# Griffin and dilated-attention encoder in one kernel: gate weights on GpSimd's queue and loaded earlier, side transfers at estimated ends, a table load counted

## The chip, the cores and the metric

The kernel runs as one launch on one core of a Trainium2 chip. The metric is the device time of the launch in microseconds, the median of several runs. The core has five queues that take instructions in order: PE (TensorE, the matrix unit), ACT (ScalarE), DVE (VectorE), POOL (GpSimd) and SP, which only issues transfers here. POOL issues transfers too. SBUF is the on-chip memory of 128 partitions, PSUM the eight banks that PE writes.

## The reference

An encoder trunk of two layers on x of 512 tokens by 1024 channels, in float32. Layer 0 mixes tokens with a recurrent block, layer 1 with dilated window attention; a gated feed-forward block with a 3-tap convolution follows each. The change touches layer 0's mixer alone:

```python
def rglru_mixer(x, w_in, conv_w, conv_b, w_a, b_a, w_x, b_x, lam, w_out):
    gate, u = jnp.split(x @ w_in, 2, axis=-1)               # 1280 channels each
    u = depthwise_conv(u, conv_w, conv_b, LRU_CONV_W // 2)  # 4 taps over tokens
    ub = u.reshape(B, S, LRU_BLOCKS, LRU_BLOCK_W)           # 16 blocks of 80 channels
    h_fwd = rglru_scan(u, ub, w_a[0], b_a[0], w_x[0], b_x[0], lam[0], False)
    h_bwd = rglru_scan(u, ub, w_a[1], b_a[1], w_x[1], b_x[1], lam[1], True)
    y = jax.nn.gelu(gate) * (h_fwd + h_bwd).astype(x.dtype)
    return y @ w_out
def rglru_scan(u, ub, w_a, b_a, w_x, b_x, lam, reverse):
    r = jax.nn.sigmoid(jnp.einsum('bsnc,ncd->bsnd', ub, w_a).reshape(B, S, D_RNN) + b_a)
    i = jax.nn.sigmoid(jnp.einsum('bsnc,ncd->bsnd', ub, w_x).reshape(B, S, D_RNN) + b_x)
    log_a = -LRU_C * jax.nn.softplus(-lam.astype(jnp.float32)) * r
    a = jnp.exp(log_a)
    inp = jnp.sqrt(-jnp.expm1(2.0 * log_a)) * (i * u.astype(jnp.float32))
    _, h = lax.associative_scan(lru_combine, (a, inp), axis=1, reverse=reverse)
    return h
```

## The kernel before, in words

**Precision.** Each operand of a matmul is split into a high part (`whi`, `xhi`, rounded) and a low part (`wlo`, `xlo`, the rest), and a product is three passes (`passes`, L270 to L273): high by high, high by low, low by high. A weight tile of 128 by 1024 is loaded raw by SP (`wraw`, L214 or L220); the high part is made by ACT (L184), or, for some tiles, loaded a second time by POOL's queue, which rounds on the way (`rounded`, L212 and L219); the low part is a subtraction on DVE (L189 to L192).

**Units.** The stage works on 1280 channels as ten tiles t of 128. For each there is a unit u (its columns of x @ w_in; 24 matmuls), a unit g (the four gates, forward and backward; one PSUM bank each) and a unit y (the gelu branch, 24 matmuls). `SEQ` (L515) is their order, and with index from 0 it is also the order of their weight tiles:

```python
SEQ = "u0 u1 u2 u3 g0 u4 g1 y0 y1 u5 g2 u6 g3 y2 y3 u7 g4 u8 g5 y4 y5 u9 g6 g7 y6 y7 g8 g9 y8 y9"
```

Then comes the output product with w_out (`token_phase`, L408): ten steps k over y's tiles, each for eight PSUM banks. The first five k run one after the other over all banks (24 matmuls each); the last five are run bank by bank. It needs y's high and low part of tile k (`turned`, L753). After it the feed-forward block starts.

**Gates.** A block of 80 channels doesn't fit a tile of 128, so a gate unit reads its own tile of u and, for the channels that a block shares with the tile before or after, a side operand (`make_side`, L601): some rows of the neighbours' u, copied by SP from SBUF to SBUF, in four or eight small pieces (L608; t mod 5 is 0, 2 or 4, "stacked") or two of 256 KB (L612, L613). It is issued by the low part of the neighbour (`low`, L589), and waits on SP for its source. The gate's weights are a tile of zeros (`zero`, L157, a memset on POOL, for the first three on DVE) into which `add_gates` (L231) copies blocks of w_a and w_x. These pieces wait in `moves`, one deque for each gate; each tick sends one on SP's queue, lowest gate first (`next_move`, L151), and what is left goes at the gate's split (`split_to`, L174).

**How far ahead.** Unit n calls `weights(n)`: tiles up to n + 3 are split, those up to n + 6 are loaded (`RGA = [6, 3]`, L518).

**The planner.** The program is one list for each queue, written by a planner that counts ticks (`tick`, L320) of `TICK` = 0.69 us. A u or y unit has 8 ticks; a gate has 4 if stacked, otherwise 8. Elementwise work is put in as pieces with an engine, a rank, a cost and what they need (`piece`, L287). At each tick `pump` (L300) emits pieces in order of rank, as long as the engine's booked time is at most 1.4 us (`SLK`) ahead of the clock and what they need is due by then. Work outside the pieces is booked where it is emitted: 1.05 for a conversion on ACT, 0.68 for a sigmoid, 0.72 for a tanh, so 4 x 0.68 + 2 x 0.72 = 4.16 us for a gate unit. `need` (L306) emits whatever is left, by rank, until a wanted key is there.

For a tile t the pieces are: rank 0, the convolution (first step on ACT L576, three taps on DVE L581), u's high part on ACT (L587) and low part on DVE (L590), and the gelu of a pair of y units (L727); rank 1, i = i x u on DVE (L658), the exponentials of a pair (L674), squares (L678) and w on DVE (L681), the roots of a pair (L686); rank 2, m, f, b and h on DVE (the input product L689, two scans L694 and L698, their sum L702); rank 3, y's product on DVE (L736), its high part on ACT (L741) and its low part on DVE (L744).

**Tiles.** SBUF work tiles come from an arena of 40 (L36), handed out first in, first out: a new tile waits for the last use of the one that had its place.

At the start of the stage POOL computes the decay rates, a series of some twenty small operations (`decay_rates`, L531).

Of the kernel before, what the change touches and what calls it, by code (L numbers as in the profile page):

```python
# [10 lines left out]
F32 = mybir.dt.float32  # L11
F32R = mybir.dt.float32r
# [10 lines left out]
FIRST = 2  # L23
TURN_AT, TURN_RG = (2, 2), (0, 1)
ZEROED = 3
POOL_LO = True


# [7 lines left out]
class Arena:  # L36
# [16 lines left out]
    def put(self, t):  # L53
        self.free.append(self.of.pop(id(t))[0])
# [3 lines left out]
def encoder(ctx: ExitStack, tc: tile.TileContext, x, ln_g, ln_b, rg_w_in, rg_conv_w, rg_conv_b,  # L58
            rg_w_a, rg_b_a, rg_w_x, rg_b_x, rg_lam, rg_w_out, at_w_qkv, at_w_o, ff_w_up,
            ff_conv_w, ff_conv_b, ff_w_down, out):  # L60
    nc = tc.nc
# [81 lines left out]
    loaders = []  # L143
    raws, his, parts = {}, {}, {}
    rounded = {}
    side_low = set()
    at = {"load": 0, "split": 0}
    gates = []
    moves = {}

# [6 lines left out]
    def zero(j, eng):  # L157
        raws[j] = sb.get([128, 1024], F32, "wraw")
        eng.memset(raws[j], 0.0)

    def load_to(i):
        while at["load"] <= min(i, len(loaders) - 1):
            j = at["load"]
            if j in gates and j not in raws:
                zero(j, nc.gpsimd)
            if j not in raws:
                raws[j] = sb.get([128, 1024], F32, "wraw")
            loaders[j](raws[j])
            if j in rounded:
                his[j] = sb.get([128, 1024], F32R, "whi")  # L170
                rounded[j](his[j])
            at["load"] += 1

    def split_to(i, pool=False):  # L174
        while at["split"] <= min(i, len(loaders) - 1):
# [55 lines left out]
    def add_gates(t):  # L231
        f0 = 128 * t
        blocks = []
        at_row = {tin: (n, row) for n, (tin, row, _) in enumerate(stacked(t) or [])}
        if at_row:
            side_low.add(len(loaders))
        for blk in range(f0 // BW, (f0 + 127) // BW + 1):
            c0, c1 = max(BW * blk, f0), min(BW * blk + BW, f0 + 128)
            for q, tin in ((0, t), (1, t + 1), (1, t - 1)):
                r0, r1 = max(BW * blk, 128 * tin), min(BW * blk + BW, 128 * tin + 128)  # L240
                if r0 < r1:
                    blocks.append((blk, q, r0, r1, tin, c0, c1))

        def go(raw):
            v = raw.rearrange("p (d a q c) -> p d a q c", d=2, a=2, q=2)
            moves[j] = todo = deque()
            for blk, q, r0, r1, tin, c0, c1 in blocks:
                n = r1 - r0
                for a, w in ((0, rg_w_a), (1, rg_w_x)):
                    src = (w[0, :, blk, r0 - BW * blk:r1 - BW * blk, c0 - BW * blk:c1 - BW * blk]  # L250
                           .rearrange("d r c -> r d c"))
                    dst = lambda p, n: v[p:p + n, :, a, q, c0 - f0:c1 - f0]
                    if not (q and at_row):
                        todo.append((dst(r0 - 128 * tin, n), src))
                    elif n == 32:

                        for d in range(2):
                            sd = src[:, d]
                            todo.append((dst(0, 96)[:, d],
                                         bass.AP(tensor=sd.tensor, offset=sd.offset, ap=[[0, 3]] + [list(x) for x in sd.ap])))  # L260
                    else:
                        m, row = at_row[tin]
                        for z in range(3):
                            todo.append((dst(r0 - 128 * tin - row + 16 * m + 32 * z, n), src))

        j = len(loaders)
        gates.append(j)
        loaders.append(go)
# [31 lines left out]
    def pump():  # L300
        now = clock[0] * TICK
        for eng in ("s", "v"):
            while side_work[eng] and booked[eng] <= now + SLK and take(eng, now + SLK):
                pass

    def need(*keys):  # L306
        for key in keys:
            while key not in due:
                assert take("s", 1e9) | take("v", 1e9), key


    queues = []
    later = []
    clock, free_at, gap = [0], [0], [GAP]
    order = itertools.count()
# [4 lines left out]
    def tick():  # L320
        clock[0] += 1
        if moves:
            next_move()
        pump()
        while later and later[0][0] <= clock[0]:
            heapq.heappop(later)[2]()
        if clock[0] >= free_at[0]:
            for q in queues:
                if q and q[0][0](clock[0]):
                    q.popleft()[1]()  # L330
                    free_at[0] = clock[0] + gap[0]
                    return
# [182 lines left out]
    SEQ = "u0 u1 u2 u3 g0 u4 g1 y0 y1 u5 g2 u6 g3 y2 y3 u7 g4 u8 g5 y4 y5 u9 g6 g7 y6 y7 g8 g9 y8 y9"  # L515
    SEQ = [(u[0], int(u[1])) for u in SEQ.split()]
    RTAIL = 5
    RGA = [6, 3]  # L518

    def add_rglru():  # L520
        for kind, t in SEQ:
# [37 lines left out]
    def rglru(i0, turn_params, load_next):  # L559
# [8 lines left out]
        def conv(t, b):  # L568
            if t % 2 == 0:
                u32[t] = u32[t + 1] = sb.get([128, 2, 512], F32, "u32")  # L570
                left[t] = 2
            u = u32[t][:, t % 2]
            c = lambda k: tab[:, k * NR + t:k * NR + t + 1]

            def first():
                nc.scalar.activation(u, b, AF.Identity, bias=tab[:, CB + t:CB + t + 1], scale=c(2))  # L576

            def taps():
                for k, sh in ((0, -2), (1, -1), (3, 1)):
                    d0, d1 = max(0, -sh), 512 - max(0, sh)  # L580
                    nc.vector.scalar_tensor_tensor(u[:, d0:d1], b[:, d0 + sh:d1 + sh], c(k), u[:, d0:d1],  # L581
                                                   op0=OP.mult, op1=OP.add)
                ps.put(b)

            def high():
                uhl[t] = pair("u")
                nc.scalar.activation(uhl[t][:, 0], u, AF.Copy)  # L587

            def low():  # L589
                nc.vector.tensor_tensor(uhl[t][:, 1], u, f(uhl[t][:, 0]), OP.subtract)  # L590
                if t % 5:
                    make_side(t - 1)
                if t % 5 == 4:
                    make_side(t)

            piece("s", 0, 0.76, ("c", t), (), first)
            piece("v", 0, 2.25, ("u", t), (("c", t),), taps)
            piece("s", 0, 0.63, ("uh", t), (("u", t),), high)
            piece("v", 0, 0.69, ("ul", t), (("uh", t),), low)

        def make_side(t):  # L601
# [8 lines left out]
            else:  # L610
                sides[t] = v = pair("side")
                nc.sync.dma_start(f(v[0:64]), f(uhl[t + 1][0:64]))  # L612
                nc.sync.dma_start(f(v[64:128]), f(uhl[t - 1][64:128]))  # L613

        r, ii, th, y = {}, {}, {}, {}
        it = iter(range(i0, i0 + 3 * NR))
        ahead[:] = RGA
# [5 lines left out]

        def g_unit(t):
            need(("ul", max(t - 1, 0)), ("ul", t), ("ul", min(t + 1, NR - 1)))
            sd = sides.pop(t)
            i = next(it)
            v = [w.rearrange("p (m q c) -> p m q c", m=4, q=2) for w in weights(i)]
            r[t] = sb.get([128, 2, 512], F32, "r")
            ii[t] = sb.get([128, 2, 512], F32, "i")  # L630
            th[t] = sb.get([128, 2, 512], F32, "th")
            for m in range(4):
                b = bank("gate")
                passes(b, [w[:, m, 0, :] for w in v], [uhl[t][:, 0], uhl[t][:, 1]], True, False)
                if stacked(t):
                    nc.tensor.matmul(b, v[0][:, m, 1, :], sd, start=False, stop=True)
                else:
                    tick()
                    passes(b, [w[:, m, 1, :] for w in v], [sd[:, 0], sd[:, 1]], False, True)
                tick()  # L640
                d = m // 2
                dst, bias = ((r[t], BA), (ii[t], BX))[m % 2]
                nc.scalar.activation(dst[:, d], b, AF.Sigmoid, bias=tab[:, bias + d * NR + t:bias + d * NR + t + 1])
                book("s", 0.68)
                ps.put(b)
                if m % 2 == 0:
                    nc.scalar.activation(th[t][:, d], r[t][:, d], AF.Tanh, scale=p8[:, d * NR + t:d * NR + t + 1])
                    book("s", 0.72)
            due["g", t] = booked["s"]
            done(i)  # L650
            sb.put(sd)
            if t:
                sb.put(uhl[t - 1])
            if t == NR - 1:
                sb.put(uhl[t])

            def gated():
                nc.vector.tensor_tensor(ii[t], ii[t], u32[t][:, t % 2][:, None, :].to_broadcast([128, 2, 512]), OP.mult)  # L658
                left[t - t % 2] -= 1
                if not left[t - t % 2]:  # L660
                    sb.put(u32[t])

            piece("v", 1, 1.22, ("i", t), (("g", t),), gated)
            if t % 2:
                decay(t - 1, t)
# [97 lines left out]
        load_next()  # L763
        for kind, t in SEQ[FIRST:]:
            {"u": u_unit, "g": g_unit, "y": y_unit}[kind](t)
        i = next(it, i0 + 3 * NR)
        xt.clear()
        load_x()
# [510 lines left out]
```

## Time and profile before

| | |
|---|---|
| median of 3 runs | 1553.0 us (1551.12 to 1556.37) |
| profiled execution | 1549.37 us |
| its span | 1547.6 us |
| mean granted clock of TensorE | 0.995 |
| PE, DVE, ACT, POOL busy | 98%, 60%, 42%, 10% |

The profile is of one execution. Its time is 1.8 us more than its span, for what lies around the span, and 3.6 us below the median of the runs. The granted clock is a share of 2.4 GHz. PE is busy nearly all of the time, so the rows below are those around its few idle stretches. A bracket at a row's end gives the idle time before the instruction and what ended it. SPq is a transfer's issue on SP's queue; its time is that of issuing alone.

### The profile page before, as it was taken

How to read it: one execution, taken by the hardware profiler on the slowest of the kernel's cores; microseconds unless marked ns; L12 is line 12 of the kernel's file. 1: busy time of each engine (PE TensorE's matmuls, PEld its weight loads, DVE VectorE, ACT ScalarE, POOL GpSimd, SP SyncE). 2: the span in 40 equal slices, each digit the busy share in tenths (PEclk: the TensorE clock that was granted, in tenths of full speed). 3: DMA queues.
4: the chain of work that ended last, by engine and by line, in shares of the span. 5: the costliest groups of instructions: out<-in, count | busy, mean ns of one | idle time of the engine just before them, and what ended most of it. 6: DMA issues, size and time to landing. Idle time of an engine off the chain costs nothing.

```text
span 1547.6 us, 20989 instructions
## 1 busy us (share of the span) xinstructions
PE 1521.2 (98%) x8078; PEld 1308.0 (85%) x8078; DVE 922.5 (60%) x1324; ACT 653.2 (42%) x1053; POOL 149.5 (10%) x372
## 2 busy tenths in 40 slices
PE   9998999999999999999999999999999999999998
PEld 8787789888888889889889889989889888888886
DVE  7585986554544245685686577568657545455225
ACT  5787813333333212553554455355442333333210
POOL 3110102000000002012012011101202000000001
PEclk9999999999999999999999999999999999999999
DMA  7865943232223321343434334434344222223321
GB/s 219 189 138 133 322 129 109 82 96 82 83 90 127 131 74 55 95 137 123 118 87 155 86 102 132 128 82 133 127 131 122 87 84 82 82 82 109 136 69 55
DMA packets 230785, 178.09 MB, mean 115 GB/s; under 512 B 19582, under 2 KB 206236, under 8 KB 230684
## 3 DMA queue, kind: packets, MB, share of 16 engines
q1 hardware_dynamic: 213372, 159.91, 34.6%
q0 software_dynamic: 17152, 16.78, 4.4%
q8 instruction: 64, 1.05, 0.3%
q14 instruction: 37, 0.30, 0.1%
q10 hardware_dynamic: 160, 0.06, 0.0%
HBM read 149.96 MB, written 2.10 MB: 98 GB/s over the span
## 4 chain that ended last, share of the span: by engine, by line
PE 89%; ACT 4%; DVE 3%; DMA 2%; issue 1%; SPq 1%; DVEq 0%; ACTq 0%
PE v L272 23%; PE o L272 20%; PE qk L272 15%; PE g L272 15%; PE u L272 2%; PE gb L272 2%; PE gate L272 2%; PE tP L1031 2%; PE oT L1059 1%; PE oT L1056 1%; PE s L926 1%; PE s L925 1%; PE tx L394 1%; PE k L272 1%; DVE wlo L192 1%
## 5 line engine op out<-in xcount | busy, mean ns | idle before, releaser
L192 DVE TENSOR_TENSOR wlo<-wraw,whi 128x1024 fp32r<-128x1024 f32 x241 | 292.7, 1224 | 198.2 <-ACT whi L184 168.4
L184 ACT ACTIVATE whi<-wraw 128x1024 fp32r<-128x1024 f32 x228 | 237.6, 1053 | 120.7 <-PE o L272 102.9
L272 PE MATMUL o<-whi,h 128*128 128x512 f32 x704 | 217.1, 389 | 0.0
L272 PEld LDWEIGHTS o<-whi,h 128*128 128x128 f32 x704 | 132.1, 188 | 27.3
L272 PE MATMUL qk<-xhi,whi 128*128 128x512 f32 x352 | 145.3, 413 | 0.0
L272 PE MATMUL v<-xhi,whi 128*128 128x512 f32 (+1 forms) x384 | 142.6, 371 | 0.0
L272 PE MATMUL v<-xlo,whi 128*128 128x512 f32 (+1 forms) x384 | 142.6, 371 | 0.0
L272 PE MATMUL v<-xhi,wlo 128*128 128x512 f32 (+1 forms) x384 | 142.6, 371 | 0.0
L272 PE MATMUL qk<-xlo,whi 128*128 128x512 f32 x352 | 138.2, 393 | 0.0
L272 PE MATMUL qk<-xhi,wlo 128*128 128x512 f32 x352 | 137.9, 392 | 0.0
L272 PE MATMUL o<-wlo,h 128*128 128x512 f32 x352 | 136.9, 389 | 0.0
L272 PE MATMUL g<-xhi,whi 128*128 128x512 f32 (+1 forms) x352 | 133.7, 380 | 0.0
L272 PE MATMUL g<-xlo,whi 128*128 128x512 f32 (+1 forms) x352 | 133.6, 379 | 0.0
L272 PE MATMUL g<-xhi,wlo 128*128 128x512 f32 (+1 forms) x352 | 133.5, 379 | 0.0
L272 PE MATMUL v<-whi,xhi 128*128 128x256 f32 x352 | 101.2, 288 | 0.0
L272 PE MATMUL v<-whi,xlo 128*128 128x256 f32 x352 | 99.7, 283 | 0.0
L272 PE MATMUL v<-wlo,xhi 128*128 128x256 f32 x352 | 99.6, 283 | 0.0
L475 DVE SCALAR_TENSOR_TENSOR t<-g,fft,t 128x511 f32<-128x511 f32 x44 | 33.0, 750 | 111.5 <-ACT t L473 111.2
L956 ACT ACTIVATE P<-P,stats 128x256 f32<-128x256 f32 x128 | 63.6, 498 | 78.9 <-DVE stats L954 78.9
L473 ACT ACTIVATE t<-g,fft 128x512 f32<-128x512 f32 x44 | 34.4, 781 | 132.8 <-PE g L272 122.5
L272 PEld LDWEIGHTS v<-xhi,wlo 128*128 128x128 f32 x384 | 72.4, 188 | 12.5
L272 PEld LDWEIGHTS v<-xlo,whi 128*128 128x128 f32 x384 | 72.3, 188 | 12.6
(228 smaller groups left out, 3086.0 us busy)
## 6 DMA issues: line engine op xcount, KB each, us to landing
wraw<-in_ff_w_up_dram SPq DMA_DIRECT2D x88, 512.0 KB
wraw<-in_at_w_qkv_dram SPq DMA_DIRECT2D x72, 512.0 KB
wraw<-in_ff_w_down_dram SPq DMA_DIRECT2D x44, 512.0 KB
wraw<-in_rg_w_in_dram SPq DMA_DIRECT2D x20, 512.0 KB
V<-vst SPq DMA_DIRECT2D x128, 64.0 KB
whi<-in_rg_w_in_dram POOLq DMA_DIRECT2D x14, 512.0 KB, 5.1
k<-k SPq DMA_DIRECT2D x48, 128.0 KB
kl<-kl SPq DMA_DIRECT2D x48, 128.0 KB
```

The lines of the kernel that those rows point to most:

```text
L184: nc.scalar.activation(hi, raw, AF.Copy)
L192: (nc.gpsimd if pool else nc.vector).tensor_tensor(lo, raw, f(hi), OP.subtract)
L272: nc.tensor.matmul(o, lhs[a], rhs[b], start=start and n == 0, stop=stop and n == 2, skip_group_check=skip)
L394: nc.tensor.transpose(b[:, 128 * k:128 * k + 128], xt[t][:, 128 * (4 * q + k):128 * (4 * q + k) + 128], ident)
L473: nc.scalar.activation(t1, bg, AF.Identity, bias=tab[:, 3 * NF + fi:3 * NF + fi + 1], scale=tab[:, NF + fi:NF + fi + 1])
L475: nc.vector.scalar_tensor_tensor(t1[:, 1:], bg[:, :511], tab[:, fi:fi + 1], t1[:, 1:], op0=OP.mult, op1=OP.add)
L925: nc.tensor.matmul(b[:, c], qa[:, h, c], ka[:, h, c], start=True, stop=False)
L926: nc.tensor.matmul(b[:, c], qa[:, h, c], kl[:, h, c], start=False, stop=True)
L956: nc.scalar.activation(P[:, b, :], P[:, b, :], AF.Exp, bias=st[:, w, 0, h, b:b + 1], scale=0.125, accum_out=st[:, w, 1, h, b:b + 1])
L1031: nc.tensor.transpose(tb[:, 128 * n:128 * n + 128], a, ident)
L1056: nc.tensor.matmul(ov0, v(0, s), pt[:, n, 0:256].rearrange("p (b r i) -> p r b i", b=2, r=4), start=(s == 0 and n == 0), stop=False, skip_ ...
L1059: nc.tensor.matmul(ov[:, s, :], v(g, s), pt[:, n, 128 + 128 * g:256 + 128 * g], start=False, stop=(s == 3 and n == 1 and g == 2), skip_gro ...
```

## The change

Four things, all in the recurrent stage:

1. For gates t of 3 and more the w_x pieces are no longer put into `moves`; they are issued on GpSimd's queue when the gate's tile is loaded.
2. The gate tiles g3 to g7 (`gates[3:-2]`) are loaded up to nine units ahead instead of six; g8 and g9 as before.
3. A side transfer is no longer issued with its source's low part. It is put into a list, and sent at the first tick at which the source's planned end has passed, or when its gate unit begins.
4. The first sigmoid of a gate unit books 1.96 us of ACT instead of 0.68, a table load of 1.28 more; the gate books 5.44. No instruction is added by this.

```diff
+RGA, GATES_AHEAD = [6, 3], 3
...
+    def load(j):
+        if j in loaded:
+            return
+        loaded.add(j)
+        if j in gates and j not in raws:
+            zero(j, nc.gpsimd)
+        if j not in raws:
+            raws[j] = sb.get([128, 1024], F32, "wraw")
+        loaders[j](raws[j])
+        if j in rounded:
+            his[j] = sb.get([128, 1024], F32R, "whi")
+            rounded[j](his[j])
+
     def load_to(i):
         while at["load"] <= min(i, len(loaders) - 1):
...
+            load(at["load"])
             at["load"] += 1
+        if ahead[0] == RGA[0]:
+            for j in gates[ZEROED:-2]:
+                if i < j <= i + GATES_AHEAD:
+                    load(j)
...
+                    put = todo.append if a == 0 or t < ZEROED else lambda m: nc.gpsimd.dma_start(*m)
                     if not (q and at_row):
-                        todo.append((dst(r0 - 128 * tin, n), src))
+                        put((dst(r0 - 128 * tin, n), src))
...
         pump()
+        for fn in at_each:
+            fn()
...
                 if t % 5:
-                    make_side(t - 1)
+                    waiting.append((t - 1, ("ul", t)))
                 if t % 5 == 4:
-                    make_side(t)
+                    waiting.append((t, ("ul", t)))
...
+        waiting = deque()
+
+        def moved(limit):
+            while waiting and due[waiting[0][1]] <= limit:
+                make_side(waiting.popleft()[0])
+
+        at_each.append(lambda: moved(clock[0] * TICK))
...
             need(("ul", max(t - 1, 0)), ("ul", t), ("ul", min(t + 1, NR - 1)))
+            while t not in sides:
+                make_side(waiting.popleft()[0])
             sd = sides.pop(t)
...
-                book("s", 0.68)
+                book("s", 0.68 if m else 1.96)
```

## Rows read from the trace of the kernel before

**Rows 1.** The page: busy time of the engines over the whole span
```profile
PE 1521.2 (98%) x8078; PEld 1308.0 (85%) x8078; DVE 922.5 (60%) x1324; ACT 653.2 (42%) x1053; POOL 149.5 (10%) x372
```

**Rows 2.** Waits of PE in the first 400 us (total, times, longest)
```profile
PE gate L272 <- ACT r L643: 4.4, 1, 4.4
...
PE gate L272 <- DMA side<-u: 3.7, 1, 3.7
...
PE o L272 <- ACT ga L727: 1.2, 1, 1.2
...
PE gate L636 <- DMA side<-u: 0.9, 1, 0.9
```

**Rows 3.** The chain that ended last: start, us, what
```profile
41.89 6.40 DMA side<-u
...
48.43 6.40 PE gate L272 x21
...
54.83 10.88 PE gb L272 x48
...
128.48 2.67 DMA wraw<-in_rg_w_x_dram
...
143.56 1.65 PE gate L272 x3
...
145.64 11.59 PE gb L272 x48
```

**Rows 4.** Timeline of SP's queue: start, us, operation, count
```profile
29.81 2.83 SPq L608 DMA_DIRECT2D side<-u  x4
...
49.49 1.51 SPq L153 DMA_DIRECT2D wraw<-in_rg_w_a_dram  x3
...
99.69 1.60 SPq L153 DMA_DIRECT2D wraw<-in_rg_w_x_dram  x1
...
109.92 0.52 SPq L612 DMA_DIRECT2D side<-u  x1
...
120.45 5.03 SPq L608 DMA_DIRECT2D side<-u  x8
```

**Rows 5.** Timeline of POOL
```profile
31.51 2.92 POOL L212 DMA_DIRECT2D whi<-in_rg_w_in_dram  x3
...
34.39 1.00 POOL L159 MEMSET wraw<- 128x1024 f32 x1
...
189.81 0.53 POOL L219 DMA_DIRECT2D whi<-in_rg_w_out_dram  x1 [2.04 <-PE o L272]
```

**Rows 6.** Timeline of PE at g0's first use of its side operand
```profile
35.42 0.47 PE L636 MATMUL gate<-side,whi 128*128 128x512 f32 x1 [0.86 <-DMA side<-u]
```

**Rows 7.** Timeline of ACT
```profile
71.98 1.28 ACT L643 ACT_TABLE_LOAD   x1
...
73.28 0.69 ACT L643 ACTIVATE r<-gate,rgt 128x512 f32<-128x512 f32 x1
...
77.11 0.62 ACT L587 ACTIVATE u<-u 128x512 fp32r<-128x512 f32 x1
...
140.23 0.76 ACT L576 ACTIVATE u<-u,rgt 128x512 f32<-128x512 f32 x1
...
151.94 1.05 ACT L184 ACTIVATE whi<-wraw 128x1024 fp32r<-128x1024 f32 x1
```

**Rows 8.** Timeline of DVE
```profile
142.41 2.31 DVE L581 SCALAR_TENSOR_TENSOR u<-u,rgt,u 128x510 f32<-128x510 f32 x3
...
174.70 1.23 DVE L689 TENSOR_TENSOR th<-th,i 128x1024 f32<-128x1024 f32 x1
...
178.95 1.22 DVE L689 TENSOR_TENSOR th<-th,i 128x1024 f32<-128x1024 f32 x1
```

**Rows 9.** Timeline of PE: first and last instructions of the output product
```profile
177.01 0.39 PE L272 MATMUL o<-whi,y 128*128 128x512 f32 x1
...
234.50 1.03 PE L394 MATMUL tx<-ident,x 128*128 128x128 f32 x8
```

More of the change, by code (lines that the diff above doesn't have):

```diff
@@ L147, in encoder @@
     at = {"load": 0, "split": 0}
+    loaded = set()
     gates = []
@@ L159, in zero @@
         eng.memset(raws[j], 0.0)
+    def load(j):
[10 more added lines that the diff above has]
+            rounded[j](his[j])
     def load_to(i):
         while at["load"] <= min(i, len(loaders) - 1):
[L163 to L171, printed above, removed]
+            load(at["load"])
             at["load"] += 1
+        if ahead[0] == RGA[0]:
+            for j in gates[ZEROED:-2]:
+                if i < j <= i + GATES_AHEAD:
+                    load(j)
     def split_to(i, pool=False):
@@ L258, in go @@
                             sd = src[:, d]
-                            todo.append((dst(0, 96)[:, d],
-                                         bass.AP(tensor=sd.tensor, offset=sd.offset, ap=[[0, 3]] + [list(x) for x in sd.ap])))
+                            put((dst(0, 96)[:, d],
+                                 bass.AP(tensor=sd.tensor, offset=sd.offset, ap=[[0, 3]] + [list(x) for x in sd.ap])))
                     else:
@@ L263, in go @@
                         for z in range(3):
-                            todo.append((dst(r0 - 128 * tin - row + 16 * m + 32 * z, n), src))
+                            put((dst(r0 - 128 * tin - row + 16 * m + 32 * z, n), src))
         j = len(loaders)
@@ L312, in encoder @@
     queues = []
+    at_each = []
     later = []
@@ L517, in encoder @@
     RTAIL = 5
-    RGA = [6, 3]
     def add_rglru():
@@ L765, in rglru @@
             {"u": u_unit, "g": g_unit, "y": y_unit}[kind](t)
+        at_each.clear()
         i = next(it, i0 + 3 * NR)
```

## The prediction

> **What bounds the kernel now.** I read the page first: PE is busy 1521.2 of 1547.6 us [rows 1], so a change to one stage can only gain what PE idles there, or lose what it makes PE idle. The waits of PE over the first 400 us come next; the recurrent stage is the first 235 us of them. It has four stalls [rows 2]: 0.9 us at g0 and 3.7 us at g1, both for side transfers; 4.4 us at g7, for a PSUM bank that ACT's sigmoids hold; 1.2 us in the output product. In the chain the long stalls cost more than their idle time, as the granted clock falls to 1.2 GHz after them: 21 matmuls take 6.40 us after the first, where 48 take 10.88 (0.227 each), so 1.6 us are lost; after the second 52 matmuls take 13.67 us from 143.56 on, 1.9 us too many [rows 3].
>
> What causes the g7 stall stands further back. ACT waits for the last w_x piece of g7's weights, which lands at 131.15 [rows 3], since SP issued it late: SP's queue stands still from 101.3 to 109.92 before side 6, whose source isn't ready, and then takes 5.03 us for the eight pieces of side 7, with g7's pieces behind both [rows 4]. This is what the change is aimed at. The output product runs from 177.01 to 234.50, 57.5 us [rows 9]; its 240 matmuls and a turn of 0.8 need 55.2, so it loses 2.3.
>
> **The change, part by part.** The order in which instructions enter the queues is fixed by the planner's constants, so it can be walked by hand. For the kernel before the walk gives the order that the timelines have.
>
> **(A) Gates nine ahead: g0.** At u3 the planner now loads up to unit 9 and then g3 (unit 12). No older pieces are pending, so the five ticks of u3 put g3's five w_a pieces on SP, ahead of the four of side 0, which are now issued at g0's start. Those pieces write a tile that POOL zeroes, and POOL comes to nothing new before 31.51, when the decay series ends; then two whi loads at 0.97 (three take 2.92) and the memset of 1.00 [rows 5]: 34.45. Five w_a pieces at 0.50 (three take 1.51) end at 37.0, side 0's four issues (2.83) at 39.8 [rows 4]. Side 0 was used 2.78 us after its last issue, at 35.42 [rows 6]; now at 42.6. That is +7.2 us, and a stall of 8 us will lower the clock: I take 1.7, between 1.6 and 1.9. For the landing the far bound is side 1's: 5.80 after its second issue of 0.60 [rows 3]; that would add 3.0. A landing faster than 2.67 [rows 3] has no row. **+8.9.**
>
> **g1** loses its stall, 3.7 + 1.6 = 5.3, as PE comes later: g0's other 13 matmuls take 3.0 + 1.7, u4 5.4, g1's first three 0.7, so PE wants side 1 at 53.4. The planner now emits g0's product i0 before u2's low part: the last sigmoid ends at 48.1, i0 49.3, low part 50.0, two issues 51.2, landing at 54.0 by 2.78 or 57.0 by 5.80. The loads that filled the queues at 42 are by then done, so I take 2.78: a stall of 0.6. **-4.7** (-1.7 by the other end).
>
> **(B) w_x on GpSimd's queue.** Thirty-five pieces (g3 to g9) leave SP, which frees 35 x 0.5 = 17 us of it, and come to POOL at 0.53 to 0.97 each [rows 5], 19 to 34 us, beside an engine busy 149.5 us of the whole span [rows 1]. Behind them on POOL stand whi loads. Units 13 and 14 bring the longest run, g6 and g7 with 13 pieces (at most 13 us), wanted 50 us later; g8's and g9's nine come some 20 us before their conversion. I cost them at nothing; without that cover they'd cost what g7 costs now.
>
> **(C) Sides at their source's estimated end.** Sides 3 to 7 no longer hold up the weights, and g6's and g7's w_a pieces leave SP in y2 and y3. g7 is ready long before it is wanted: 4.4 + 1.9 come back. **-6.3.**
>
> **(D) Table load counted: u9.** A gate unit now books 5.44 us of ACT instead of 4.16; u9's first step is emitted only when the booked time is at most 1.4 us ahead of the clock. At the second tick of g6 ACT is booked to 124.7 at 122.8, so it just misses; before, it fitted, one tick earlier, and ran at 140.23, before g6's sigmoids [rows 7]. From there g6, g7 and two conversions book 2 x 5.44 + 2 x 1.05 = 13.0 us in 12 ticks (8.3 us), so the door stays shut until the second tick of y7. u9's low part is then forced at g8's start and side 8 is issued there.
>
> Call G the time when PE ends g7. g6's first bank is full at G - 7.7. ACT then needs a load of 1.28, eight sigmoids and four tanh (2 x 3.83, the stretch from 73.28 to 77.11) and the conversions of g8 and g9 (about 1 each) [rows 7]: G + 3.3. Behind g9's conversion DVE has, in this order, g9's low part, m, f and b of unit 5, i7, y8's low part (1.2 each, 1.4 for g9) and u9's taps, 2.31 [rows 8]: G + 13.0. u9's high and low parts, with h5 and p4 between them, take 1.8; two issues at 0.63 (eight take 5.03) [rows 4] 1.3; landing 2.8: G + 18.9. PE, after y6, y7 and three matmuls, wants it at G + 11.6. Stall 7.3 (10.3 with a landing of 5.80), clock 1.7. **+9.0.**
>
> **(E) The same booking at the end.** Work of rank 3 (y's high and low parts) starves on the booked ACT, and y3's low part is emitted only when PE asks for k = 3 of the output product; asking empties DVE's backlog by rank, so all scans of units 6 to 9 stand before it. The root of 6 and 7 now stands behind the gelu of y9, PE's last unit, which ends at Y: gelu 0.7, load 1.28, root 1.0, so m6 starts at Y + 3. m6, w8 and w9 follow; then wo5's low part needs a tile. Following the 40 tiles first in, first out (the same count puts POOL's load at 189.81 behind a unit of PE's output product, as the row has it [rows 5]), it gets one that PE frees at the end of k = 1, Y + 11. From there: two low parts 2.4, f, b, h of unit 6 3.0, three blocks of m, f, b, h at 4.25 (174.70 to 178.95) [rows 8] 12.75, y3 0.6: Y + 29.8. PE reaches k = 3 at Y + 16.3. Stall 13.5, or 9.5 if no tile is waited for; clock 1.7. The losses of 2.3 that the stage has now go. **+12.9.**
>
> On a table load: ACT's next activation starts 1.30 us after the load's start [rows 7]. The Trainium skill (ScalarE: Activation LUTs, What ACT_TABLE_LOAD costs) puts a switch of tables at about 2.66 us with a drain. By it (D) and (E), with one load each on their path, would be some 2.8 us dearer together; the rows show no drain, so the sum keeps 1.28.
>
> **Sum:** 8.9 - 4.7 - 6.3 + 9.0 + 12.9 = **+19.8**. The profiled execution took 1549.4 us, so 1569.2. The median of the runs, 1553.0, is 3.6 above it; a median of the changed kernel is forecast at **1572.8**.
>
> **Rivals.**
> *Only the repair counts (faster).* Place: g7, price 6.3 us, 1546.7. It decides if the planner's order costs nothing: if side 8 lands before G + 11.6 and y3's low part is done before Y + 16.3. For it: before, ACT was idle often enough, and the estimate runs behind PE (four ticks of a stacked gate count 2.8 us and take 3.6). Against: both late chains are DVE work in a fixed order, 7 and 13 us too long, and g0's pieces wait for a memset that can't be earlier. Chance 0.05.
> *The early cost without the late ones.* If (D) and (E) are hidden but (A) and (C) hold: 8.9 - 4.7 - 6.3 = -2.1, 1550.9, no difference to see. 0.05.
> *g0 isn't delayed.* If the memset were not behind the decay series, (A) and g1 drop out: -6.3 + 9.0 + 12.9 = +15.6, 1568.6. 0.15.
> *Slow landings.* If sides 0, 1 and 8 land as side 1 does now: +3 each, 1581.8. 0.15.
> *The change does less than it says.* It can't leave the order as it is, since the booking is a constant; a g3 that isn't loaded early is the rival above.
>
> **How the numbers follow.** My forecast has 0.6, the rivals with later ends 0.3, so slower by over 0.3% (4.7 us, about what a measurement of this kernel can tell) has 0.90; within 0.05; faster 0.05. The low end takes (E) without the tile and (A) without its delay, 1572.8 - 4.0 - 4.2 = 1564.6, rounded down; the high end takes the slow landings, 1582.
>
> **What would show it.** Right: PE waits of some 8 us at g0 for side 0, 7 at g8 for side 8 and 13 in the output product for y3's low part on DVE; none at g7; in SP's timeline g3's w_a pieces before side 0, with a stand until about 34.5; on ACT u9's first step after g9's conversion; a granted clock below full speed just after those waits. Wrong: g8 entered without a wait, or a DVE without a run of scans between the second and the fourth k of the output product.

## The result and the profile after

The changed kernel takes **1574.3 us** (median of 4 runs, 1571.27 to 1577.17) against 1553.2 (1551.12 to 1556.37) for the kernel before in the same series: 1.0134 times as long, 95% interval 1.0103 to 1.0164. The forecast was 1572.8, range 1564 to 1582, slower.

The profiled execution took 1571.72 us, its span is 1569.9, 22.3 more than before. The page says where not to look: PE does the same work in the same busy time, and what is added is idle time. The mean granted clock fell from 0.995 to 0.988.

```profile
PE 1522.0 (97%) x8078; PEld 1309.1 (83%) x8078; DVE 923.0 (59%) x1324; ACT 653.2 (42%) x1052; POOL 170.0 (11%) x407
```

The waits of PE over the first 400 us (total, times, longest). Against [rows 2], ACT's wait at g7 and the one in the output product are gone. Three others have come: 10.8 us for side 0 at g0, 7.1 for side 8 at g8 (the other second of 8.1 is g1's), and 12.7 in the output product.

```profile
PE o L284 <- DVE y L767: 12.7, 1, 12.7
PE gate L659 <- DMA side<-u: 10.8, 1, 10.8
PE gate L284 <- DMA side<-u: 8.1, 2, 7.1
```

The timeline of PE puts them in place (start, us, operation, count, idle time before and what ended it); first in the row is g0, then g1, g8 and k = 3 of the output product.

```profile
45.29 0.77 PE L659 MATMUL gate<-side,whi 128*128 128x512 f32 x1 [10.81 <-DMA side<-u]
...
58.20 0.70 PE L284 MATMUL gate<-side,whi 128*128 128x512 f32 x2 [0.95 <-DMA side<-u]
...
167.15 1.19 PE L284 MATMUL gate<-side,whi 128*128 128x512 f32 x2 [7.15 <-DMA side<-u]
...
217.71 1.22 PE L284 MATMUL o<-whi,y 128*128 128x512 f32 x2 [12.72 <-DVE y L767]
```

**g0.** The timeline of POOL has the memset behind the decay series, as [rows 5] let one expect; then POOL's five new w_x issues take 2.87.

```profile
33.21 1.01 POOL L161 MEMSET wraw<- 128x1024 f32 x1
34.51 2.87 POOL L264 DMA_DIRECT2D wraw<-in_rg_w_x_dram  x5 [0.29 <-POOL wraw L161]
```

The timeline of SP's queue beside it: nothing is issued from 26.82 until the memset is done; then come g3's five w_a pieces, and only then side 0. The last two rows are side 8.

```profile
25.80 1.02 SPq L225 DMA_DIRECT2D wraw<-in_rg_w_in_dram  x2
34.25 2.59 SPq L155 DMA_DIRECT2D wraw<-in_rg_w_a_dram  x5
36.93 2.54 SPq L622 DMA_DIRECT2D side<-u  x4
...
162.60 0.56 SPq L626 DMA_DIRECT2D side<-u  x1
163.22 0.59 SPq L627 DMA_DIRECT2D side<-u  x1
```

**What a stall costs beyond its idle time** is in the chain (start, us, what). g8's 24 matmuls take 7.25 us, where the 48 at 188.22 show 0.227 each, so 5.44: 1.8 are lost to the clock. The 136 of the output product behind its wait take 32.95 where 30.9 would do: 2.1 lost. A side transfer's time there counts from the start of its last issue.

```profile
38.88 6.27 DMA side<-u
...
58.20 5.00 PE gate L284 x21
...
163.22 3.79 DMA side<-u
...
167.15 7.25 PE gate L284 x24
...
188.22 10.89 PE o L284 x48
...
217.71 32.95 PE o L284 x136
```

After g0's stall it is more. In the timeline of PE, g0's other 13 matmuls run from the first use of the side to u4's first matmul in 5.68 us (45.29 to 50.97):

```profile
50.97 0.39 PE L284 MATMUL u<-xhi,whi 128*128 128x512 f32 x1
```

In the kernel before the same stretch took 3.03 (35.42 [rows 6] to 38.45), so 2.65 are lost:

```profile
38.45 0.39 PE L272 MATMUL u<-xhi,whi 128*128 128x512 f32 x1
```

The windows (stretch, its length, busy time and count of PE, PEld, DVE, ACT, POOL, then granted clock, DMA share, GB/s) show the clock at half, its 1.2 GHz level, through the stall and still in the four microseconds after it.

```profile
38.00:42.00 4.00, 0.00 (x0) 0.00 (x0) 0.10 (x1) 0.00 (x0) 3.70 (x6) 0.50 1.07 214
42.00:46.00 4.00, 0.71 (x2) 0.65 (x3) 0.00 (x0) 0.00 (x0) 1.08 (x2) 0.50 1.25 272
46.00:50.00 4.00, 4.00 (x11) 3.14 (x10) 0.00 (x0) 2.60 (x4) 0.00 (x0) 0.50 0.26 57
```

**g8 and the output product.** The timeline of ACT shows u9's first step at 151.16, directly behind g9's conversion (it ran at 140.23 in [rows 7]); its high part waits until 160.86.

```profile
150.21 1.05 ACT L195 ACTIVATE whi<-wraw 128x1024 fp32r<-128x1024 f32 x1
151.16 0.77 ACT L590 ACTIVATE u<-u,rgt 128x512 f32<-128x512 f32 x1
...
160.86 0.63 ACT L601 ACTIVATE u<-u 128x512 fp32r<-128x512 f32 x1 [5.05 <-issue]
```

In the timeline of DVE the taps of u9 come last of a run, and its low part ends at 162.58; side 8 is issued then. Later, m of unit 6 starts at 191.27, wo5's low part gets its tile at 199.14, and from there four units' scans run without a gap until y3's low part at 216.98, which PE has been waiting for since 205.0.

```profile
158.46 2.31 DVE L595 SCALAR_TENSOR_TENSOR u<-u,rgt,u 128x510 f32<-128x510 f32 x3
161.89 0.69 DVE L604 TENSOR_TENSOR u<-u,u 128x512 fp32r<-128x512 f32 x1
...
191.27 1.23 DVE L712 TENSOR_TENSOR th<-th,i 128x1024 f32<-128x1024 f32 x1 [6.62 <-ACT th L709]
...
199.14 1.22 DVE L203 TENSOR_TENSOR wlo<-wraw,whi 128x1024 fp32r<-128x1024 f32 x1 [1.93 <-PE o L284]
...
216.98 0.68 DVE L767 TENSOR_TENSOR y<-ga,y 128x512 fp32r<-128x512 f32 x1
```

### The profile page after: what moved, and what is told of

Same layout as the page of the kernel before. It is cut to its first block, busy times and chain, and to the rows that moved or that the text cites. A ratio compares the mean times of both kernels' runs of the same rounds, so it can differ in the third digit from the quotient of the medians.

```text
span 1569.9 us, 21003 instructions
## 1 busy us (share of the span) xinstructions
PE 1522.0 (97%) x8078; PEld 1309.1 (83%) x8078; DVE 923.0 (59%) x1324; ACT 653.2 (42%) x1052; POOL 170.0 (11%) x407
## 4 chain that ended last, share of the span: by engine, by line
PE 93%; DVE 3%; DMA 1%; ACT 1%; issue 1%; SPq 0%; DVEq 0%; ACTq 0%
PE v L284 24%; PE o L284 21%; PE qk L284 15%; PE g L284 15%; PE u L284 3%; PE gb L284 3%; PE gate L284 2%; PE tP L1055 2%; PE oT L1083 1%; PE oT L1080 1%; PE s L950 1%; DMA side<-u 1%; PE s L949 1%; PE tx L409 1%; PE k L284 1%
## 5 line engine op out<-in xcount | busy, mean ns | idle before, releaser
L488 ACT ACTIVATE t<-g,fft 128x512 f32<-128x512 f32 x44 | 34.3, 780 | 133.1 <-PE g L284 122.8
L284 PEld LDWEIGHTS v<-xhi,wlo 128*128 128x128 f32 x384 | 72.4, 189 | 12.7
L284 PEld LDWEIGHTS v<-xhi,whi 128*128 128x128 f32 x384 | 72.4, 188 | 12.3
```

Of the source, the lines that this page charges most:

```text
L284: nc.tensor.matmul(o, lhs[a], rhs[b], start=start and n == 0, stop=stop and n == 2, skip_group_check=skip)
L488: nc.scalar.activation(t1, bg, AF.Identity, bias=tab[:, 3 * NF + fi:3 * NF + fi + 1], scale=tab[:, NF + fi:NF + fi + 1])
```

## Experiments

Two measures are given for each kernel. One is its time against the kernel before in the same series. The other, "stage end", is the time in the profile at which PE starts the first product of the feed-forward block (235.78 before, 259.49 after, so 23.7 later). It holds everything that the change can touch and leaves out the rest of the span, which is 1311.8 before and between 1310.4 and 1315.0 in all the others. It also holds the start of the kernel, where PE waits for x: g0 wants its side at 34.3 to 34.9 us, in experiment 7 at 35.5. Below, kernel n is that of experiment n.

| kernel | time, us | ratio, 95% interval | stage end, us |
|---|---|---|---|
| after | 1574.3 | 1.0134, 1.0103 to 1.0164 | 259.49 |
| after without the booking | 1549.5 | 0.9982, 0.9967 to 0.9997 | 234.08 |
| before with the booking | 1575.0 | 1.0164, 1.0132 to 1.0196 | 263.67 |
| after without early gates | 1564.8 | 1.0090, 1.0062 to 1.0117 | 251.51 |
| w_x and sides only | 1539.2 | 0.9922, 0.9896 to 0.9947 | 228.02 |
| w_x only | 1542.4 | 0.9947, 0.9926 to 0.9968 | 230.57 |
| sides only | 1547.0 | 0.9979, 0.9968 to 0.9990 | 233.40 |
| after, u9 forced before g6 | 1564.8 | 1.0093, 1.0071 to 1.0115 | 250.45 |
| after, y3 forced before g8 | 1565.3 | 1.0096, 1.0073 to 1.0119 | 250.00 |
| no booking, early gates from g4 | 1541.1 | 0.9936, 0.9920 to 0.9952 | 227.48 |
| after, g3's tile zeroed on DVE | 1567.7 | 1.0105, 1.0089 to 1.0120 | 255.67 |
| w_x and sides, u2 before g0 | 1538.2 | 0.9914, 0.9901 to 0.9927 | 224.84 |

The medians of the kernel before in the four series were 1553.2 (the changed kernel), 1552.1 (experiments 1 to 4), 1549.0 (5 to 8) and 1552.0 (9 to 11). So times of different series can differ by some 4 us for no reason in the kernel, and across series the ratios and the stage ends say more.

**1. The booking taken out of the changed kernel.**

```diff
-                book("s", 0.68 if m else 1.96)
+                book("s", 0.68)
```

> The change without its fourth part: the first sigmoid books 0.68 us again. My theory (two of the three new stalls come from the planner's bookkeeping alone, the third, at g0, from g3's early load): the waits at g8 and in the output product go, the one at g0 of some 10 us stays, g7 stays without a wait; 25 us less than the changed kernel, so 1549 us (1545 to 1555). Rival (the early loads and the pieces on GpSimd's queue hold up transfers that g8 and the output product wait for): those two waits stay, and the time stays within 5 us of 1574.

Measured 1549.5; the stage ends 25.4 us earlier. Its waits of PE have neither g8 nor the output product any more:

```profile
PE gate L659 <- DMA side<-u: 10.1, 1, 10.1
...
PE gate L284 <- DMA side<-u: 0.4, 1, 0.4
```

So both late stalls hang on a number in the planner, while the work that ACT does is the same.

**2. The booking alone, in the kernel before.**

```diff
-                book("s", 0.68)
+                book("s", 0.68 if m else 1.96)
```

> The kernel before with the fourth part alone: the first sigmoid books 1.96 us, no other edit. My theory: the planner's new order is enough for waits at g8 (7 to 10 us) and before k = 3 of the output product (13 us), while the wait at g7 remains in part (2 to 4 us); 21 us more than before, so 1574 us (1568 to 1580). Rival (the booking only shifts work that other engines cover, the loss is in the queues): within 5 us of 1553.

Measured 1575.0. The 12.7 in the output product is there again, and g8 waits 10.6 (the other 2.9 of the listed 13.5 are g1's); ACT's wait at g7 grew to 4.9, from 4.4, where less was expected.

```profile
PE gate L272 <- DMA side<-u: 13.5, 2, 10.6
PE o L272 <- DVE y L744: 12.7, 1, 12.7
```

The two late stalls need nothing of the rest of the change.

**3. No early gates.**

```diff
-        if ahead[0] == RGA[0]:
-            for j in gates[ZEROED:-2]:
-                if i < j <= i + GATES_AHEAD:
-                    load(j)
```

> The change without its second part: gates are loaded six units ahead as before. My theory: g3's pieces no longer stand before side 0, so the wait at g0 falls from 10.8 us to about 1 and the one at g1 grows back to 2 to 4; the waits at g8 and k = 3 stay at 7 and 13 us; some 7 us less than the changed kernel, 1567 us (1562 to 1571). Rival (side 0 is late because it is now issued at g0's start): the wait at g0 stays near 10 us and the time within 3 us of 1574.

Measured 1564.8, 9.5 below the changed kernel (8.0 at the stage end). The wait at g0 is 2.0 in place of 10.8 and the one at g1 1.4, where 1 and 2 to 4 were expected; those at g8 (7.2) and in the output product (12.7) stand. Sides are still sent from the list here, so the list isn't what holds side 0 up.

**4. w_x and sides only** (experiments 1 and 3 together).

> The change's first and third part alone: w_x pieces on GpSimd's queue and sides at their source's estimated end; no early gates, no booking. My theory: the wait at g7 goes and no new one comes but those at g0 and g1 that the kernel before has; the output product loses nothing; 11 us less than before, 1542 us (1538 to 1547), faster than both kernels. Rival (pieces on GpSimd's queue cost more than they free): at or above 1553.

Measured 1539.2, 12.9 below the kernel before and the fastest so far. Of the waits of its gates and its output product only those are left that the kernel before has at g0 and g1:

```profile
PE gate L280 <- DMA side<-u: 3.8, 1, 3.8
...
PE gate L655 <- DMA side<-u: 1.0, 1, 1.0
```

The stage ends 7.8 earlier: 6.3 of it is g7, and the output product, 56.6 us from its first matmul to the stage end against 58.8, gave back the rest and more than g1 took. The difference of the medians is 5 larger than that; the profiled execution here is the slowest of this kernel's five, and that of the kernel before lay 3.6 below its median, so what the medians differ by beyond the stage can't be placed.

**5 and 6. Each of the two alone**, from kernel 4. w_x only:

```diff
-                    waiting.append((t - 1, ("ul", t)))
+                    make_side(t - 1)
...
-                    waiting.append((t, ("ul", t)))
+                    make_side(t)
```

> The kernel before with w_x pieces on GpSimd's queue alone (sides issued with their source's low part, gates six ahead, no booking). My theory: SP has 35 pieces fewer, and side 7's eight no longer have w_x pieces of g7 behind them, so the wait at g7 goes and the time is that of w_x and sides together: 1541 us (1537 to 1546). Rival (the repair comes from the sides' later issue): near 1553, with a wait of some 4 us at g7.

Sides only:

```diff
-                    put = todo.append if a == 0 or t < ZEROED else lambda m: nc.gpsimd.dma_start(*m)
+                    put = todo.append
```

> The kernel before with the sides at their source's estimated end alone. My theory: SP no longer stands before side 6, so g7's pieces land earlier, but all pieces are still SP's: the wait at g7 falls to about 1 us, and a small one stays in the output product; 6 us less than before, 1547 us (1543 to 1551). Rival (sides alone are enough): 1541, as with w_x on GpSimd's queue.

Measured 1542.4 and 1547.0, the first 5.2 and the second 2.4 earlier at the stage end. Both times lie in the expected ranges, but partly by luck: the kernel before took 1549.0 in this series, so they are 6.7 and 2.0 less, where 12 and 6 were expected. Neither lists the wait at g7, so each repairs g7 by itself; about 1 us was expected there for the second. Sides only leaves a wait of 1.9 for ACT in the output product, which runs 60.4 us.

**7 and 8. The two late steps, each forced earlier in the changed kernel**, at the start of a gate unit:

```diff
+            if t == 6:
+                need(("ul", 9))
```

> The changed kernel, but u9's four pieces are emitted before g6 whatever ACT has booked (one need call). This takes away the cause that I give for the wait at g8 and leaves the rest of the booking. My theory: no wait at g8, the one before k = 3 stays at 13 to 14 us and the one at g0 at 10.8; 9 us less than the changed kernel, 1565 us (1560 to 1570). Rival (PE only trades the waits: what it doesn't lose at g8 it loses before k = 3): the wait before k = 3 grows to some 20 us and the time stays within 4 us of 1574.

```diff
+            if t == 8:
+                need(("yl", 3))
```

> The changed kernel, but y2's and y3's last pieces are emitted before g8 (one need call), so that y3's low part no longer stands behind all scans. This takes away the cause that I give for the wait before k = 3. My theory: that wait goes, one of about 3 us comes at the last k for a weight tile's low part, the waits at g0 and g8 stay (11 and 7 to 9 us); 9 us less than the changed kernel, 1565 us (1560 to 1570). Rival (k = 4 then waits as long, since y4's low part stands behind the same scans): within 4 us of 1574, with a wait of some 10 us before k = 4.

Measured 1564.8 and 1565.3. Against the changed kernel, which ran in another series, that is 9.6 and 9.0 less; by the ratios it is some 6 for each, and at the stage end 9.0 and 9.5. So the 9 expected fits the profiles, while the times alone don't tell it from 6. With u9 forced, the waits of PE have g8 no more (1.4 is g1's), and the output product waits as before:

```profile
PE o L284 <- DVE y L769: 12.6, 1, 12.6
PE gate L661 <- DMA side<-u: 9.8, 1, 9.8
...
PE gate L284 <- DMA side<-u: 1.4, 1, 1.4
```

With y3 forced, the product no longer waits for y3, but for a low part of weights, 2.6 at most, and g8 waits 2 us longer. u9 isn't later for it: side 8's last issue ends 3.8 us after PE wants the side, as in the changed kernel. But side 8 is used 5.3 us after that issue here and 3.3 there; why its landing took longer isn't shown.

```profile
PE gate L284 <- DMA side<-u: 9.9, 2, 9.1
PE gate L661 <- DMA side<-u: 9.7, 1, 9.7
PE o L284 <- DVE wlo L203: 2.8, 2, 2.6
```

The two stalls are separate: the first taken away leaves the second at its size.

**9. Early gates, without g3** (and without the booking).

```diff
-            for j in gates[ZEROED:-2]:
+            for j in gates[ZEROED + 1:-2]:
```

> The change without the booking, and with g4 to g7 loaded nine units ahead instead of g3 to g7. My theory: only g3's early load delays side 0, so the wait at g0 falls to about 1 us and the time is that of w_x and sides without early gates, 1540 us (1536 to 1544). Rival (loading any gate nine ahead costs, by the tiles it holds or by its transfers): 1545 or more, with waits after g1.

Measured 1541.1, stage end 227.48, 6.6 before that of kernel 1. g0 waits 2.0 (about 1 expected). Of the early loading only g3's costs: nine units ahead is harmless for g4 to g7. It brings nothing clear either: it is 0.5 ahead of kernel 4 at the stage end, of which 0.4 were there before g0.

**10. g3's tile zeroed on DVE**, in the changed kernel.

```diff
-            zero(j, nc.gpsimd)
+            zero(j, nc.vector if j == gates[ZEROED] else nc.gpsimd)
```

> The changed kernel with g3's tile zeroed by DVE instead of POOL. My theory: the memset no longer waits for the decay series on POOL, so g3's w_a pieces and side 0 leave SP some 5 us earlier; the wait at g0 falls from 10.8 us to about 5 and the time to 1569 us (1565 to 1573). Rival (the pieces before side 0 cost by their number or their transfers, not by the memset): the wait at g0 stays within 2 us of 10.8.

Measured 1567.7, 3.8 less than the changed kernel at the stage end; g0 waits 6.8, not 10.8:

```profile
PE gate L659 <- DMA side<-u: 6.8, 1, 6.8
```

With the memset done at 31.25, the timeline of SP's queue has g3's pieces and side 0 three microseconds earlier, where five were expected:

```profile
31.28 2.60 SPq L155 DMA_DIRECT2D wraw<-in_rg_w_a_dram  x5
33.98 2.52 SPq L622 DMA_DIRECT2D side<-u  x4
```

So the memset's place behind POOL's decay series makes 3 of the 10 us by which g0's wait grew. A fourth is a landing of 4.8 (last issue done at 36.5, used at 41.28) in place of 5.8; that one need not be the memset's, as kernels 1, 7 and 8, with the memset on POOL, land in 5.1, 4.7 and 4.7. The other 6, against [rows 4] and [rows 6], are the five issues ahead of side 0 (2.6), the stand until 31.28 (1.5 later than side 0's first issue before), and a landing 2.0 longer than 2.78.

**11. u2's low part before g0**, added to kernel 4 to take its wait at g1 away.

```diff
+            if t == 0:
+                need(("ul", 2))
```

> w_x pieces on GpSimd's queue and sides at their source's estimated end, as in the fastest kernel so far, and u2's last pieces emitted before g0 (one need call), so that side 1 leaves before ACT is busy with g0's sigmoids. My theory: the wait at g1 of 3.8 us and the low clock behind it go, the wait at g0 stays at about 1 us; 1534 us (1530 to 1538). Rival (side 1 then lands among the loads of that time and is no earlier, or holds side 0 up): 1539 or more.

Measured 1538.2, the lowest of all kernels run, but just above the expected range, 1530 to 1538, and 4 above the expected 1534. The wait at g1 is gone. The chain of its first 70 us shows what was given back: side 0 lands 4.18 after its last issue began (3.32 in kernel 4), g0 waits 2.2, and its other matmuls run at the lower clock, 36.65 to 41.45, 4.80 in place of 3.23 in kernel 4 (35.76 to 38.99).

```profile
32.23 4.18 DMA side<-u
...
36.65 0.50 PE gate L657
...
41.45 5.45 PE u L280 x24
```

At the stage end it is 3.2 us ahead of kernel 4: by the rows, 5.7 gained at g1 (3.81 of wait and 1.9 of clock) and 2.8 lost at g0 (1.2 and 1.6) make 2.9 of it; the other 0.3 were there before g0. In time, 1 us between two series, the two are not told apart.

## Why the prediction was right

The sign, the places and the causes were as forecast; the size at g0 was not. By step, in us:

| step | forecast | measured in the profile |
|---|---|---|
| (A) g0 | +8.9 | +12.6: idle 10.81 less 0.86, clock 2.65 |
| g1 | -4.7 | -4.15: 0.95 and 5.00 against 3.70 and 6.40 |
| (B) w_x on POOL | 0 | none seen |
| (C) g7 | -6.3 | -6.3: no wait |
| (D) g8 | +9.0 | +8.95: idle 7.15, clock 1.8 |
| (E) output product | +12.9 | +12.7: 71.4 to the stage end against 58.8 |
| sum | +19.8 | +23.8; +23.7 at the stage end, +22.3 in the span |

**(A) is the term that was mis-sized.** Its issues were right to half a microsecond: memset done at 34.22 (34.45 forecast), pieces at 36.84 (37.0), side 0's issues at 39.47 (39.8). The landing was not: 5.8 us, the far bound, where 2.78 from [rows 6] was taken. Part of the 5.8 is this one execution's: kernels 1, 7 and 8 run the same order up to g0, and side 0 is used 5.1, 4.7 and 4.7 after the end of its last issue there. So the term was some 2 us too small each time, and 3 in this profile. The reason given for side 1, that the loads are done by then, should have been asked at side 0 too. But that the loads make the difference isn't shown. From side 0's first issue to its use GpSimd's queue has a DMA share of 76.3% (36.9 to 45.3), and 45.0% in the kernel before (29.8 to 35.4); over the landing alone it has 97.3% (39.5 to 45.3) and, before, 90.1% (32.6 to 35.4), so the row taken was not a quiet one.

The other 0.95 is the clock, 2.65 in place of 1.7. The bounds came from stalls of 3.7 and 4.4 us, and this one is 10.8 long; yet length alone doesn't set it, since the same stretch at g0 lost 1.8 after a wait of 9.78 (experiment 7) and 2.65 after one of 9.74 (experiment 8).

**(D) and (E)** came out by the working of the prediction. For g8, PE wanted side 8 at 160.0, so G is 148.4; the taps of u9 end at 160.7, G + 12.3 (13.0 forecast), and side 8 was used at G + 18.75 (18.9), as a landing of 3.3 after the last issue (2.78) used up what DVE was quicker. For the product, with Y at 188.2: m of unit 6 at 191.27 (191.2), wo5's low part at 199.14 (199.2), y3 ready at 217.66 (218.0). The root of 6 and 7 does stand behind y9's gelu, with a table load of 1.28 and its first activation 1.29 after that load's start:

```profile
188.26 0.60 ACT L750 ACTIVATE ga<-gb 128x512 f32<-128x512 f32 x1 [1.97 <-PE gb L284]
188.88 1.28 ACT L709 ACT_TABLE_LOAD   x1
190.17 2.01 ACT L709 ACTIVATE th<-th 128x1024 f32<-128x1024 f32 x2
```

The Trainium skill (ScalarE: Activation LUTs, What ACT_TABLE_LOAD costs) puts a switch at about 2.66; m would by that figure, as an estimate, have come 1.4 later, and the trace doesn't agree: m started within 0.1 of the forecast, which counted 1.28. Experiments 1 and 2 show that the booking makes both; 7 and 8, that they are two.

**(B)** POOL's busy time rose by 20.5 us for 35 more instructions, 0.59 each, without a wait of PE behind them, and in experiment 5 w_x on POOL alone brings 5.2 of the 7.8 us that it brings with the sides. One part stays open: g3's five w_x pieces are among the loads beside which side 0 lands late. No run had g3 early with w_x on SP, so their share of that landing isn't known.

**Rivals.** "Only the repair counts" fell with the two late stalls. "g0 isn't delayed" fell too, and its condition was drawn too wide: in experiment 10 the memset is out from behind the decay series, and g0 still waits 6.8, so (A) and g1 don't drop out with it. "Slow landings" held for side 0 in full, +3.0 in this profile, and only by some 0.5 each for sides 1 and 8 (3.3 after the last issue's end in both, against 2.78).

**Luck.** The median is only 1.5 us above the forecast, but the terms are 4.0 too low together. In the profile 1.4 of that came back in the rest of the span, which the change can't touch, and 1.0 since the profiled execution lay 2.6 below its median, not 3.6.

**What the parts are worth.** The booking costs 25 us, g3's early loading 8.4 (kernel 9 against 1) to 9.5 (experiment 3; at the stage end 6.6 and 8.0), and w_x and sides together give 13 (8 of it seen at the stage end). A version that keeps those two alone beats both kernels, with 1539.2; with u2's low part before g0 it is 1538.2.

## What to carry to other kernels

A planner's cost is a control of the order, and a truer cost is not a better order: before one is raised, walk what the emptier budget starves, down to the last unit, since a step that is only emitted when it is asked for has everything of higher rank in front of it. Before a load is moved ahead on an in-order queue, look for what its first transfer waits for: here a memset on another, busy engine held up a transfer that PE needed, and the pieces themselves stood before it. The price of a landing or of a stall is a range and not one row: side 0 landed in 2.8 to 5.8 us over these kernels, and g0's waits of some 10 us cost 1.8 to 2.65 more in clock.

## What was not expected of the hardware

Of the same kind of transfer, four side pieces of 64 KB, the last took 3.3 us in experiment 4 and 6.3 in the changed kernel from the start of its issue, though it was issued from SP's queue and the loads beside it are mostly GpSimd's.

Short stalls of about 2 us ended either way for the clock. After 1.96 us at g0 in experiment 9 the stretch is granted full speed, after 1.97 in experiment 3 the next stretch falls to the lower level; after 2.10 in experiment 2 and 2.13 in experiment 5 it stayed full, after 2.24 in experiment 11 it fell. The windows from 36 to 40 us, first of experiment 9:

```profile
36.00:38.00 2.00, 1.75 (x8) 1.50 (x9) 1.88 (x2) 1.15 (x2) 2.00 (x4) 1.00 1.53 283
38.00:40.00 2.00, 2.00 (x11) 1.65 (x10) 0.00 (x0) 1.97 (x4) 1.98 (x3) 1.00 1.51 327
```

then of experiment 3:

```profile
36.00:38.00 2.00, 1.48 (x4) 1.22 (x5) 1.97 (x3) 0.69 (x1) 2.00 (x4) 0.66 1.61 300
38.00:40.00 2.00, 2.00 (x7) 1.52 (x6) 0.17 (x1) 1.41 (x2) 1.69 (x3) 0.50 1.49 318
```

What decides between them isn't seen in these rows. It makes a wait at this place worth either itself or 1.6 us more: g0's other matmuls take 3.03 in experiment 9 and 4.64 in experiments 3 and 11. That 1.6 is the larger part of what experiment 11 lost at g0.
